# Six layer norms of a two-layer decoder step: mean and squares taken from shifted features while the last products run, in place of after them

## The chip, the cores and the metric

The kernel runs on one core of one Trainium2 chip. Its time is that of the whole program on the device, in microseconds. Three runs of the kernel before took 2835.37, 2836.15 and 2839.43 us; the median, 2836.15 us, is the time before. The profiled execution is a further one.

## What is computed

One inference step of a decoder with two layers, on 1024 prompt tokens and 32 sample tokens (8 sequences of 4), 1024 features wide:

```
layer 0: mixer = sparse attention (an indexer scores all keys, the 256 best are kept)
layer 1: mixer = gated causal convolution of width 3
each layer:
  y = layer_norm(ALPHA * y + mixer(y))
  a, g = split(y @ w_up);  h = silu(causal_conv3(a) + b) * g       # 2816 features
  y = layer_norm(ALPHA * y + h @ w_down)

layer_norm(x): mu = mean(x); var = mean((x - mu)**2)
               (x - mu) * rsqrt(var + 1e-5) * gain + bias
```

All of it is fp32. The change bears on the first three of the four layer norms; the last one (`last_norm`) is another function and stays.

## The kernel before, in words

**Precision.** Each large operand is split into two fp32r parts, `hi` (ScalarE, a rounding copy, L129) and `lo` (the rest, by a subtraction on VectorE or GpSimd, L130). A product is three passes: `wh·xh`, `wh·xl`, `wl·xh` (L732, L733, L735 in `product`, L724). Weights come by DMA into `raw` on SP's queue and are split right before use (`unit`, L714). Matmuls with `allones`, in the norms, are in full fp32.

**Layout.** Activations lie with features on the partitions: `r` is 128 x 8 blocks x tokens, so a layer norm sums over 8 blocks and over the 128 partitions. Tokens are in two groups: A, 512 prompt tokens, and B, the other 512 with the 32 sample tokens, 544 columns in two halves of 272.

**Order.** First come the projections and the indexer, then the attention of A. Then A goes through the attention's output projection (`out_proj`, L794), norm 0, the FFN of layer 0, norm 1, the conv mixer, norm 2, and the beginning of the FFN of layer 1. In that time the scores, the top-k and the attention of B are a background generator (L1284): `weave` (L79 to L85) issues pieces of it between A's products according to costs written by hand, and `drain` issues what is left. After the background, B runs its own `out_proj`, norm 0, FFN, norm 1, conv, norm 2 and FFN, and the rest of A's last FFN is cut into chunks (`CHUNKS`, L19; `N0, N1, N2 = 2, 3, 4`, L49) that are issued around B's norms as cover (`stage`, L1314; L1346 to L1360): features 0 to 7 before B starts, 8 to 11 around norm 0, 12 to 15 around norm 1, 16 to 21 around norm 2.

`pipeline` (L863) runs a chunk: the up products of its features (`up`), the first up of the next chunk, then the down products (`down`, L751): for each of the 8 output blocks `d` a product over the chunk's features, which VectorE adds into `r` (L773), or, in the first chunk, combines with the residual (L782, L813). The framework orders each engine's instructions ahead of time by a priority list; on the chip every engine runs its own in that order, and waits on semaphores.

**The norm** (`norm`, L974) is called after the last `down`:

1. GpSimd adds the blocks of `r` into `s` as they come (L982, L984; in B the last one on VectorE, L987). In A the last block goes into the matmul by itself.
2. PE sums over partitions with a matrix of ones (`sums`, L957, L962), ScalarE scales that to the mean (L990).
3. VectorE subtracts it from two blocks at a time (L994), ScalarE squares them (L996), GpSimd adds the two squares (L997); in B further adds bring all into one row (L1003).
4. PE turns the squares by matmuls with one column into a variance for each token, tokens on the partitions (L1013, L1017): a column for each 128 tokens and term, four terms in A, one in B. VectorE takes it out (L1023), GpSimd raises it to the power -1/2 (L968), VectorE does a Newton step (L969 to L971).
5. VectorE makes diagonal matrices of the result (L1028), PE spreads them over the partitions (L1033), ScalarE copies (L1035), VectorE multiplies (L1038), ScalarE applies gain and bias (L1041), and the new `xh`, `xl` are split off, the second and fourth `xl` on GpSimd.

While A's part runs, PSUM is tight (`single` is true): the products and the norm's sums take turns in two banks. Later there are three double banks for products and two others for the norm.

## Time and profile before

| what | value |
|---|---|
| runs of the kernel before, median | 2836.15 us |
| the profiled execution, time | 2832.02 us |
| its span, first to last instruction | 2830.2 us |
| mean granted TensorE clock over the span | 0.968 |
| instructions in it | 43977 |
| moved by DMA | 271.57 MB |

The profile is of one execution. Its span leaves out what lies before the first and after the last instruction, 1.8 us here, and the execution is 4.1 us faster than the median. PE is TensorE, DVE VectorE, ACT ScalarE, POOL GpSimd, SP the engine that issues most DMAs. An instruction is named by engine, line of the kernel and tiles, output first: `mm<-xhA,wh` is a product in group A. PE's busy time covers instructions that overlap; the granted clock is 1.00 at the upper level and 0.5 at the lower.

### The profile page before, as it was taken

How to read it: one execution, taken by the hardware profiler on the slowest of the kernel's cores; microseconds unless marked ns; L12 is line 12 of the kernel's file. 1: busy time of each engine (PE TensorE's matmuls, PEld its weight loads, DVE VectorE, ACT ScalarE, POOL GpSimd, SP SyncE). 2: the span in 40 equal slices, each digit the busy share in tenths (PEclk: the TensorE clock that was granted, in tenths of full speed). 3: DMA queues.
4: the chain of work that ended last, by engine and by line, in shares of the span. 5: the costliest groups of instructions: out<-in, count | busy, mean ns of one | idle time of the engine just before them, and what ended most of it. 6: DMA issues, size and time to landing. Idle time of an engine off the chain costs nothing.

```text
span 2830.2 us, 43977 instructions
## 1 busy us (share of the span) xinstructions
PE 2708.3 (96%) x16441; PEld 2422.8 (86%) x16441; DVE 1807.1 (64%) x3348; ACT 1329.6 (47%) x2305; POOL 702.1 (25%) x1040
## 2 busy tenths in 40 slices
PE   7999989899999989998999999999999998999997
PEld 7789977688777778886879899999989987999996
DVE  3466576998889855677754755445664566754446
ACT  3576774766886553356632533332332234432323
POOL 4455742111222353135201300000310031200001
PEclk8999999899999979999999999999999999999999
DMA  4245543133223323322244232323222322333332
GB/s 146 63 140 137 152 140 118 53 97 91 80 78 86 106 76 125 107 71 64 65 136 142 71 90 84 89 84 108 85 83 68 99 79 75 119 90 87 89 93 72
DMA packets 144021, 271.57 MB, mean 96 GB/s; under 512 B 27712, under 2 KB 74240, under 8 KB 143168
## 3 DMA queue, kind: packets, MB, share of 16 engines
q1 hardware_dynamic: 141120, 259.32, 31.0%
q0 software_dynamic: 2688, 9.44, 1.0%
q8 instruction: 130, 2.13, 0.3%
q14 instruction: 83, 0.68, 0.1%
HBM read 245.34 MB, written 23.36 MB: 95 GB/s over the span
## 4 chain that ended last, share of the span: by engine, by line
PE 77%; DVE 9%; ACT 5%; issue 4%; DMA 3%; POOL 2%; SPq 0%; ACTq 0%; DVEq 0%; POOLq 0%
PE mm L732 15%; PE mm L735 15%; PE mm L733 15%; PE m L735 6%; PE m L732 6%; PE m L733 6%; PE pv L587 2%; DVE wl L130 2%; PE tr L583 2%; PE pj L186 2%; PE pj L187 1%; PE pj L185 1%; PE ix L319 1%; ACT tkb L422 1%; PE ix L567 1%
## 5 line engine op out<-in xcount | busy, mean ns | idle before, releaser
L129 ACT ACTIVATE wh<-raw 128x1024 fp32r<-128x1024 f32 (+2 forms) x456 | 383.7, 842 | 806.0 <-PE mm L733 605.7
L130 DVE TENSOR_TENSOR wl<-raw,wh 128x1024 fp32r<-128x1024 f32 (+2 forms) x456 | 467.8, 1027 | 280.5 <-ACT wh L129 275.5
L732 PE MATMUL mm<-xhB,wh 128*128 128x272 f32 x1920 | 520.2, 290 | 6.2 <-ACT xhB L129 6.2
L733 PE MATMUL mm<-xlB,wh 128*128 128x272 f32 x1920 | 519.0, 288 | 2.5 <-DVE xlB L130 2.5
L735 PE MATMUL mm<-xhB,wl 128*128 128x272 f32 x1920 | 398.0, 289 | 0.0
L732 PEld LDWEIGHTS mm<-xhB,wh 128*128 128x128 f32 x1920 | 363.7, 190 | 7.3 <-ACT xhB L129 7.0
L733 PEld LDWEIGHTS mm<-xlB,wh 128*128 128x128 f32 x1920 | 362.7, 189 | 3.3 <-DVE xlB L130 3.0
L735 PEld LDWEIGHTS mm<-xhB,wl 128*128 128x128 f32 x1920 | 301.2, 189 | 0.0
L732 PE MATMUL m<-xhA,wh 128*128 128x512 f32 x736 | 294.0, 402 | 6.1 <-DVE h L857 2.4
L733 PE MATMUL m<-xlA,wh 128*128 128x512 f32 x736 | 293.6, 399 | 3.3 <-DVE xlA L130 3.0
L735 PE MATMUL m<-xhA,wl 128*128 128x512 f32 x736 | 293.7, 399 | 1.5 <-DVE wl L130 1.4
L732 PE MATMUL mm<-hh,wh 128*128 128x272 f32 (+1 forms) x928 | 269.6, 307 | 8.9 <-DVE r L773 8.0
L733 PE MATMUL mm<-hl,wh 128*128 128x272 f32 (+1 forms) x928 | 268.6, 305 | 0.0
L735 PE MATMUL mm<-hh,wl 128*128 128x272 f32 (+1 forms) x928 | 220.1, 306 | 2.2 <-DVE wl L130 2.2
L732 PEld LDWEIGHTS mm<-hh,wh 128*128 128x128 f32 x928 | 175.1, 189 | 16.7 <-DVE r L773 5.9
L733 PEld LDWEIGHTS mm<-hl,wh 128*128 128x128 f32 x928 | 175.4, 189 | 6.1
L834 POOL COPY ffn_outs<-ext 128x2 f32<-128x2 f32 x44 | 25.7, 584 | 601.0 <-ACT ext L903 600.9
L732 PEld LDWEIGHTS m<-xhA,wh 128*128 128x128 f32 x736 | 140.3, 192 | 36.7 <-DVE h L857 3.0
L733 PEld LDWEIGHTS m<-xlA,wh 128*128 128x128 f32 x736 | 140.2, 191 | 33.5 <-DVE xlA L130 4.2
L735 PEld LDWEIGHTS m<-xhA,wl 128*128 128x128 f32 x736 | 140.4, 191 | 31.4 <-DVE wl L130 2.5
L185 PE MATMUL pj<-W,X 128*128 128x368 f32 (+3 forms) x480 | 154.9, 325 | 12.1 <-ACT W L129 10.3
L773 DVE TENSOR_TENSOR r<-r,mm 128x544 f32<-128x544 f32 (+1 forms) x120 | 85.1, 710 | 121.9 <-PE mm L735 121.5
(369 smaller groups left out, 5960.9 us busy)
## 6 DMA issues: line engine op xcount, KB each, us to landing
raw<-w_up SPq DMA_DIRECT2D x176, 512.0 KB, 3.6
raw<-w_down SPq DMA_DIRECT2D x128, 256.0 KB, 2.6
raw<-w_ci SPq DMA_DIRECT2D x48, 512.0 KB, 3.6
X<-xp SPq DMA_DIRECT2D x24, 512.0 KB, 3.2
raw<-w_down SPq DMA_DIRECT2D x64, 192.0 KB, 2.4
qr<-dQ SPq DMA_DIRECT2D x64, 128.0 KB, 2.9
raw<-w_ao SPq DMA_DIRECT2D x16, 512.0 KB, 3.6
raw<-w_co SPq DMA_DIRECT2D x32, 256.0 KB, 2.7
```

The costliest lines, as they stand in the source:

```text
L129: nc.scalar.activation(hi, src, AF.Copy)
L130: (nc.gpsimd if pool else nc.vector).tensor_sub(lo, src, hi.bitcast(F32))
L185: nc.tensor.matmul(p, xh[:, k, :], hi, start=(k == 0), stop=False)
L186: nc.tensor.matmul(p, xh[:, k, :], lo, start=False, stop=False)
L187: nc.tensor.matmul(p, xl[:, k, :], hi, start=False, stop=(k == 7))
L319: nc.tensor.matmul(p, Q[:, h % 8, :], K[z][:, c:c + m], start=(z == 0), stop=(z == 1))
L583: nc.tensor.transpose(p[:, 128 * j:128 * j + 128], es[j][:, 128 * c:128 * c + 128], self.ident)
L587: nc.tensor.matmul(o, V[:, c], pp[:, z], start=(c == 0 and z == 0), stop=(c == i and z == 1))
L732: nc.tensor.matmul(o, wh[:, k, :], xh[:, c:c + m], start=(k == 0), stop=False)
L733: nc.tensor.matmul(o, wh[:, k, :], xl[:, c:c + m], start=False, stop=False)
L735: nc.tensor.matmul(o, wl[:, k, :], xh[:, c:c + m], start=False, stop=(k == n - 1))
L773: nc.vector.tensor_add(rv, rv, acc)
```

## The change

A class `Norm` takes the place of `norm`. `down` calls its `each` after every block `d` of the last chunk. Up to `d = 3` GpSimd sums the blocks 0 to 3; ScalarE rounds that sum to fp32r, and one pass of a matmul gives `c`, about the mean of those 512 features, the same value in all partitions. From `d = 4` on the blocks are shifted by `c` on VectorE: the finished ones two at a time, the unfinished ones before their last product is added. ScalarE squares shifted pairs into one tile `B`, GpSimd adds the squares into `acc` and the shifted blocks into `s1`. In `finish` the remaining mean `mb` comes from `s1` by an fp32 matmul, and the variance columns have twice as many PSUM columns: sums of `s1`, and squares from `acc`, `B[:, 0]` and `B[:, 1]`. The variance is mean square less squared mean. The four pairs then lose `mb`, and the rest of the norm is as before. In `out_proj` the residual is always added in the only chunk, so blocks from 5 on are shifted inside `base`.

Beside it: `out_proj` loads the attention output in four DMAs of two blocks into `r` itself, not in eight through the two-buffer tile `h`; the background generator is put on the list when the last query tile of A is done, and what was on the list before is finished ahead of A's last two key heads; A's last FFN is cut as `LAST`, seven chunks, six features of which come before B starts, 6 to 9 around norm 0, 10 to 15 (two chunks) around norm 1.

```diff
-N0, N1, N2 = 2, 3, 4
+
+LAST = ((0, 4), (4, 2), (6, 4), (10, 4), (14, 2), (16, 3), (19, 3))
+N0, N1, N2 = 2, 3, 5
...
+class Norm:
+    def __init__(self, net, g, m):
+        self.net, self.g, self.m = net, g, m
+        self.nc, self.n = net.nc, g.n
+    def row(self, dt=F32):
+        return self.net.wk.tile([128, 544], dt, name="nr", bufs=2)[:, :self.n]
+    def two(self):
+        return self.net.wk.tile([128, 2, 544], F32, name="n", bufs=self.net.nn)[:, :, :self.n]
+    def bc(self, x):
+        return x[:, None, :].to_broadcast([128, 2, self.n])
+    def each(self, d, r, fresh):
+        nc, n = self.nc, self.n
+        one = lambda d: r[:, d, :n]
+        pair = lambda d: r[:, d:d + 2, :n]
+        shift = lambda x: nc.vector.tensor_sub(x, x, self.bc(self.c) if len(x.shape) == 3 else self.c)
+        if d == 1:
+            self.A = self.two()
+            self.acc, self.s1 = self.A[:, 0], self.A[:, 1]
+            self.s = self.acc
+            nc.gpsimd.tensor_add(self.s, one(0), one(1))
+        elif d == 2:
+            nc.gpsimd.tensor_add(self.s, self.s, one(2))
+        elif d == 3:
+            self.sr = self.row(F32R)
+            nc.gpsimd.tensor_add(self.s, self.s, one(3))
+            nc.scalar.activation(self.sr, self.s, AF.Copy)
+        elif d == 4:
+            self.c = self.row()
+            for p, cols in self.net.sums(self.g, [self.sr], self.net.allonesr):
+                nc.scalar.activation(self.c[:, cols], p, AF.Copy, scale=1.0 / 512.0)
+            shift(pair(0))
+            shift(one(4) if fresh else pair(4))
+            nc.vector.scalar_tensor_tensor(self.s1, self.c, -4.0, self.s, op0=OP.mult, op1=OP.add)
+            self.B = self.two()
+            nc.scalar.activation(self.B, pair(0), AF.Square)
+            nc.gpsimd.tensor_add(self.acc, self.B[:, 0], self.B[:, 1])
+        elif d == 5:
+            if not fresh:
+                shift(pair(6))
+            for e in (4, 5):
+                nc.gpsimd.tensor_add(self.s1, self.s1, one(e))
+            self.squares(pair(4))
+            shift(pair(2))
+        elif d == 6:
+            nc.gpsimd.tensor_add(self.s1, self.s1, one(6))
+            self.squares(pair(2))
+        elif d == 7:
+            nc.vector.tensor_add(self.s1, self.s1, one(7))
+            nc.scalar.activation(self.B, pair(6), AF.Square)
+    def squares(self, x):
+        self.nc.scalar.activation(self.B, x, AF.Square)
+        for z in range(2):
+            self.nc.gpsimd.tensor_add(self.acc, self.acc, self.B[:, z])
+    def finish(self, r):
+        nc, net, g, n, m = self.nc, self.net, self.g, self.n, self.m
+        pair = lambda d: r[:, d:d + 2, :n]
+        mb = self.row()
+        for p, cols in net.sums(g, [self.s1], net.allones):
+            nc.scalar.activation(mb[:, cols], p, AF.Copy, scale=1.0 / 1024.0)
+        tiles = [(i, c, min(128, n - c)) for i, c in enumerate(range(0, n, 128))]
+        nt = len(tiles)
+        var = net.bank()
+        nc.tensor.matmul(var[:, :2 * nt], net.allones, net.zeros[:, :2 * nt], start=True, stop=False)
+        terms = [(self.s1, nt), (self.acc, 0), (self.B[:, 0], 0), (self.B[:, 1], 0)]
+        for i, (x, o) in enumerate(terms):
+            for t, c, k in tiles[::-1]:
+                nc.tensor.matmul(var[:k, o + t:o + t + 1], x[:, c:c + k], net.allones[:, 0:1], start=False,
+                                 stop=(i == 3 and t == 0))
+        sm = net.wk.tile([128, 4, 6], F32, name="mv", bufs=2)[:, :, :nt]
+        if g.b:
+            nc.gpsimd.memset(sm, 1.0)
+        for rows, c in ((128, slice(0, 4)), (32, slice(4, 5)))[:1 + g.b]:
+            v, mean, q = sm[:rows, 0, c], sm[:rows, 3, c], sm[:rows, 2, c]
+            nc.vector.tensor_scalar(mean, var[:rows, nt:2 * nt][:, c], 1.0 / 1024.0, None, op0=OP.mult)
+            nc.vector.scalar_tensor_tensor(q, mean, -1.0, mean, op0=OP.mult, op1=OP.mult)
+            nc.vector.scalar_tensor_tensor(v, var[:rows, c], 1.0 / 1024.0, q, op0=OP.mult, op1=OP.add)
+            nc.vector.tensor_scalar(v, v, EPS, None, op0=OP.add)
+        y = net.rsqrt(sm[:, 0], sm[:, 1], sm[:, 2])
+        yb = diag = self.row()
+        for t, c, k in tiles:
+            nc.vector.tensor_scalar(diag[:k, c:c + k], net.ident[:k, :k], y[:k, t:t + 1], None, op0=OP.mult)
+        for d in range(0, 8, 2):
+            nc.vector.tensor_sub(pair(d), pair(d), self.bc(mb))
+        for c0 in range(0, n, 512):
+            p = net.bank()
+            for t, c, k in tiles:
+                if c0 <= c < c0 + 512:
+                    nc.tensor.matmul(p[:, c - c0:c - c0 + k], net.allones[:k], diag[:k, c:c + k], start=True, stop=True)
+            m_ = min(512, n - c0)
+            nc.scalar.activation(yb[:, c0:c0 + m_], p[:, :m_], AF.Copy)
+        xh, xl = net.new_x(g)
+        for d in range(0, 8, 2):
+            nc.vector.tensor_mul(pair(d), pair(d), self.bc(yb))
+            t = self.two()
+            for z in range(2):
+                nc.scalar.activation(t[:, z], r[:, d + z, :n], AF.Identity, scale=net.ln[:, m, d + z, 0:1],
+                                     bias=net.ln[:, m, d + z, 1:2])
+            net.split(xh[:, d:d + 2, :], xl[:, d:d + 2, :], t, pool=d % 4 == 2)
...
-    def down(self, g, r, hh, hl, n, src, base, apart=False):
+    def down(self, g, r, hh, hl, n, src, base, apart=False, norm=None):
...
                 base(d, rv, acc)
+            if norm:
+                norm.each(d, r, base is not None)
...
-    def out_proj(self, g):
+    def out_proj(self, g, norm):
         nc, a = self.nc, self.a
         hh, hl = self.new_x(g)
-        for d in range(8):
-            raw = self.wk.tile([128, 560], F32, name="h", bufs=2)[:, :g.n]
-            nc.sync.dma_start(raw, self.do[g.name][:, d, :])
-            self.split(hh[:, d, :], hl[:, d, :], raw)
         r = self.new_r()
+        for d in range(0, 8, 2):
+            raw = r[:, d:d + 2, :g.n]
+            nc.sync.dma_start(raw, self.do[g.name][:, d:d + 2, :])
+            self.split(hh[:, d:d + 2, :], hl[:, d:d + 2, :], raw)
 
         def base(d, rv, acc):
             xr = self.wk.tile([128, 560], F32, name="cv", bufs=2)
@@ -810,12 +928,17 @@
             else:
                 nc.sync.dma_start(xr[:, :512].rearrange("p (t c) -> p t c", t=4),
                                   a["xp"][0:4, :, d, :].rearrange("t p c -> p t c"))
-            nc.vector.scalar_tensor_tensor(rv, g.view(xr[:, :g.n]), ALPHA, acc, op0=OP.mult, op1=OP.add)
+            if d < 5:
+                nc.vector.scalar_tensor_tensor(rv, g.view(xr[:, :g.n]), ALPHA, acc, op0=OP.mult, op1=OP.add)
+            else:
+                nc.vector.scalar_tensor_tensor(rv, g.view(xr[:, :g.n]), ALPHA, g.view(norm.c), op0=OP.mult,
+                                               op1=OP.subtract)
+                nc.vector.tensor_add(rv, rv, acc)
...
-    def sums(self, g, terms):
+    def sums(self, g, terms, ones):
...
-                self.nc.tensor.matmul(p, self.allones, t[:, s], start=(i == 0), stop=(i == len(terms) - 1))
+                self.nc.tensor.matmul(p, ones, t[:, s], start=(i == 0), stop=(i == len(terms) - 1))
...
-        self.allones = pc.tile([128, 128], F32, name="allones")
-        nc.vector.memset(self.allones, 1.0)
-        self.zeros = pc.tile([128, 8], F32, name="zeros")
+        self.allonesr = pc.tile([128, 128], F32R, name="allones")
+        self.allones = self.allonesr.bitcast(F32)
+        nc.vector.tensor_scalar(self.allonesr, self.ident, 0.0, 1.0, op0=OP.mult, op1=OP.add)
+        self.zeros = pc.tile([128, 10], F32, name="zeros")
...
+            self.bg.append(background())
...
             self.weave(cost)
+        self.finish(1)
         for cost in together((self.attend(GA, T1, range(4), (2, 3)), A1), (second(), A2)):
             self.weave(cost)
-        self.drain()
-        self.bg = [background()]
         close("p1")
...
-        r = self.result(self.out_proj(GA))
-        self.norm(GA, r, 0)
+        norm = Norm(self, GA, 0)
+        norm.finish(self.result(self.out_proj(GA, norm)))
         self.fill(F0)
...
-        r = self.result(self.ffn(GA, 0))
-        self.norm(GA, r, 1)
-        r = self.result(self.conv(GA))
-        self.norm(GA, r, 2)
+        norm = Norm(self, GA, 1)
+        norm.finish(self.result(self.ffn(GA, 0, norm=norm)))
+        norm = Norm(self, GA, 2)
+        norm.finish(self.result(self.conv(GA, norm)))
         self.fill(F0)
 
-        G = self.ffn(GA, 1, CHUNKS[:N0])
+        G = self.ffn(GA, 1, LAST[:N0])
...
-        G = stage("oB", self.out_proj(GB), G, rA.append)
+        norms = [Norm(self, GB, m) for m in range(3)]
+        G = stage("oB", self.out_proj(GB, norms[0]), G, rA.append)
         r = self.result(G)
-        G = self.ffn(GA, 1, CHUNKS[N0:N1], rA[0])
+        G = self.ffn(GA, 1, LAST[N0:N1], rA[0])
         self.until(G, "begun")
-        self.norm(GB, r, 0)
+        norms[0].finish(r)
         self.until(G, "tail")
         new_r("b")
-        G = stage("fB0", self.ffn(GB, 0), G, lambda r: None)
-        F = self.ffn(GA, 1, CHUNKS[N1:N2], rA[0])
-        G = stage("fA1b", F, G, lambda r: self.norm(GB, r, 1))
-        G = stage("cB", self.conv(GB), G, lambda r: None)
-        F = self.ffn(GA, 1, CHUNKS[N2:], rA[0])
-        G = stage("fA1c", F, G, lambda r: self.norm(GB, r, 2))
+        G = stage("fB0", self.ffn(GB, 0, norm=norms[1]), G, lambda r: None)
+        F = self.ffn(GA, 1, LAST[N1:N2], rA[0])
+        G = stage("fA1b", F, G, norms[1].finish)
+        G = stage("cB", self.conv(GB, norms[2]), G, lambda r: None)
+        F = self.ffn(GA, 1, LAST[N2:], rA[0])
+        G = stage("fA1c", F, G, norms[2].finish)
```

## Rows read from the trace of the kernel before

**Rows 1.** The page, first part: an engine's busy time, its share of the span, its instructions.
```profile
PE 2708.3 (96%) x16441; PEld 2422.8 (86%) x16441; DVE 1807.1 (64%) x3348; ACT 1329.6 (47%) x2305; POOL 702.1 (25%) x1040
```
**Rows 2.** Busy time by stretches: the stretch in us from the start of the span, its length, then the busy time (and number of instructions) of PE, PEld, DVE, ACT and POOL, the granted share of the TensorE clock, the DMA share, and GB/s. Two stretches for each norm, in order A0, A1, A2, B0, B1, B2: from the last `r` to line 1023, and from there until products run densely.
```profile
474.30:494.20 19.90, 16.21 (x71) 13.32 (x69) 17.52 (x14) 11.14 (x22) 8.15 (x4) 0.77 0.18 57
494.20:531.50 37.30, 26.97 (x90) 19.40 (x88) 33.54 (x63) 28.70 (x52) 7.95 (x11) 0.71 0.06 21
990.30:1018.60 28.30, 23.34 (x104) 19.75 (x103) 14.00 (x18) 13.49 (x17) 15.96 (x24) 0.62 0.25 75
1018.60:1045.50 26.90, 23.62 (x103) 17.91 (x102) 15.25 (x28) 14.06 (x22) 19.66 (x26) 0.77 0.25 79
1283.50:1307.60 24.10, 17.62 (x89) 13.92 (x87) 18.44 (x34) 12.73 (x18) 10.62 (x8) 0.86 0.23 62
1307.60:1345.50 37.90, 31.03 (x145) 22.80 (x143) 28.70 (x64) 28.41 (x45) 21.43 (x15) 0.95 0.13 39
1547.70:1582.30 34.60, 34.60 (x158) 28.25 (x157) 24.51 (x23) 13.65 (x19) 12.71 (x10) 1.00 0.29 82
1582.30:1608.00 25.70, 23.23 (x130) 20.45 (x129) 21.81 (x30) 16.69 (x23) 10.25 (x10) 0.93 0.12 34
2030.30:2057.00 26.70, 26.70 (x123) 21.84 (x123) 21.61 (x21) 11.51 (x15) 13.79 (x10) 1.00 0.34 101
2057.00:2085.00 28.00, 21.83 (x118) 19.45 (x118) 20.58 (x27) 15.74 (x21) 8.17 (x8) 0.82 0.10 28
2302.50:2329.30 26.80, 26.80 (x123) 21.85 (x122) 21.59 (x20) 10.91 (x15) 13.27 (x9) 1.00 0.22 66
2329.30:2364.00 34.70, 26.78 (x111) 20.93 (x110) 26.50 (x39) 18.74 (x28) 9.52 (x6) 0.95 0.23 69
```
**Rows 3.** The chain of waits, for PE: what waited for what, us in total, times, the longest in us.
```profile
PE mm L732 <- DVE r L773: 8.0, 3, 3.0
PE m L1017 <- POOL n L997: 6.9, 5, 4.9
PE mm L732 <- ACT xhB L129: 6.2, 2, 5.4
```
**Rows 4.** The norm's instructions by line: how many, the shortest, median and longest duration in ns, the first and last start in us, the shapes; in the last row the number, busy us and the mean in ns.
```profile
L984 POOL TENSOR_TENSOR nr<-nr,r x30: 1252/1587/2447, 443.2 to 2299.6; 128x512 f32<-128x512 f32 x15, 128x544 f32<-128x544 f32 x15
L990 ACT ACTIVATE nr<-m x3: 597/602/604, 477.5 to 1289.9; 128x512 f32<-128x512 f32 x3
L994 DVE TENSOR_TENSOR r<-r,nr x24: 1217/1284/2452, 478.2 to 2313.0; 128x1024 f32<-128x1024 f32 x12, 128x1088 f32<-128x1088 f32 x12
L996 ACT ACTIVATE n<-r x24: 1041/1078/1120, 479.5 to 2320.0; 128x1024 f32<-128x1024 f32 x12, 128x1088 f32<-128x1088 f32 x12
L997 POOL TENSOR_TENSOR n<-n x24: 1266/1848/2412, 480.6 to 2322.1; 128x512 f32<-128x512 f32 x12, 128x544 f32<-128x544 f32 x12
L1023 DVE TENSOR_SCALAR mv<-m 128x4 f32<-128x4 f32 x3 | 0.5, 153 | 0.0
```
**Rows 5.** The instructions that write `r` in the last products ahead of A0, A1, A2 (its last six), B1 and B2, in the columns of rows 4; and the weight splits of units of three features, all of them, with busy us, mean ns and idle time before.
```profile
L813 DVE SCALAR_TENSOR_TENSOR r<-cv,m x8: 680/688/691, 434.3 to 473.6; 128x512 f32<-128x512 f32 x8
L773 DVE TENSOR_TENSOR r<-r,m x8: 667/675/687, 966.8 to 989.6; 128x512 f32<-128x512 f32 x8
L773 DVE TENSOR_TENSOR r<-r,m x6: 675/682/689, 1263.3 to 1282.8; 128x512 f32<-128x512 f32 x6
L773 DVE TENSOR_TENSOR r<-r,mm x8: 706/722/722, 2013.8 to 2029.6; 128x544 f32<-128x544 f32 x8
L773 DVE TENSOR_TENSOR r<-r,mm x8: 709/722/722, 2280.7 to 2301.7; 128x544 f32<-128x544 f32 x8
L130 DVE TENSOR_TENSOR wl<-raw,wh 128x384 fp32r<-128x384 f32 x56 | 41.3, 737 | 19.1 <-ACT wh L129 19.1
```
**Rows 6.** PE in order of time: start in us, length in us, line, operation, shapes, number merged into the row, and the idle time before it where there was any; the last row in the columns of rows 4.
```profile
473.39 1.02 PE L962 MATMUL m<-nr,allones 128*128 128x512 f32 x2
...
2055.23 1.21 PE L1017 MATMUL tr<-allones,nr 128*32 128x1 f32 x10
2056.30 0.47 PE L735 MATMUL mm<-xhA,wl 128*128 128x512 f32 x1
2056.61 0.39 PE L732 MATMUL mm<-xhA,wh 128*128 128x512 f32 x1
2056.84 0.40 PE L733 MATMUL mm<-xlA,wh 128*128 128x512 f32 x1
...
2071.93 0.82 PE L732 MATMUL mm<-xhB,wh 128*128 128x272 f32 x2 [5.37 <-ACT xhB L129]
L962 PEld LDWEIGHTS tr<-nr,allones x12: 187/188/193, 1557.5 to 2308.3; 128*128 128x128 f32 x12
```
**Rows 7.** The loads of the attention output (L799): who waited for them, us, times.
```profile
  ACT xhB L129: 9.9, 4
  ACT xhA L129: 8.3, 4
```
**Rows 8.** First, in the columns of rows 4, the background's last kind of product (`pv`); then, in the columns of rows 2, the stretch from there to the end of A's last up product, and the one between the norms B1 and B2.
```profile
L587 PE MATMUL pv<-pp,V x288: 387/394/803, 262.8 to 1432.7; 128*128 128x512 f32 x144
1433.00:1471.50 38.50, 38.31 (x169) 31.29 (x167) 22.22 (x31) 13.33 (x19) 1.89 (x6) 1.00 0.47 157
2080.00:2320.00 240.00, 240.00 (x1731) 230.44 (x1730) 123.31 (x178) 61.11 (x79) 33.59 (x43) 1.00 0.30 89
```

More of the change, by code (lines that the diff above doesn't have):

```diff
@@ L817, in out_proj @@
         yield from self.down(g, r, [hh[:, k, :] for k in range(8)], [hl[:, k, :] for k in range(8)], 8,
-                             lambda d: a["w_ao"][d], base)
+                             lambda d: a["w_ao"][d], base, norm=norm)
         return r
@@ L885, in pipeline, with ffn @@
         return r
-    def ffn(self, g, l, chunks=CHUNKS, r=None, apart=False):
+    def ffn(self, g, l, chunks=CHUNKS, r=None, apart=False, norm=None):
         nc, a = self.nc, self.a
@@ L915, in down, with conv @@
             return self.down(g, r, [h[0] for h in H], [h[1] for h in H], nf,
-                             lambda d: a["w_down"][l, d, :, f0:f0 + nf, :], base, apart and f0 + nf == NFF)
+                             lambda d: a["w_down"][l, d, :, f0:f0 + nf, :], base, apart and f0 + nf == NFF,
+                             norm if f0 + nf == NFF else None)
         return self.pipeline(g, up, chunks, down, get_r, base, 10.3)
-    def conv(self, g):
+    def conv(self, g, norm):
         nc, a = self.nc, self.a
@@ L949, in down @@
         def down(r, H, f0, nf, base):
-            return self.down(g, r, [h[0] for h in H], [h[1] for h in H], nf, lambda d: a["w_co"][d, :, f0:f0 + nf, :], base)
+            return self.down(g, r, [h[0] for h in H], [h[1] for h in H], nf, lambda d: a["w_co"][d, :, f0:f0 + nf, :], base,
+                             norm=norm if f0 == 4 else None)
         return self.pipeline(g, up, ((0, 4), (4, 4)), down, self.new_r, self.residual(g), 15.5)
```

66 lines of the change are left out of this document (removed).

## The prediction

> **What bounds the kernel now.** I read the page's busy shares first [rows 1]: TensorE is busy 2708.3 of 2830.2 us, so there is something to win only where it stands or its granted clock is low. The table by stretches [rows 2] shows where: around the six layer norms. Call them A0, A1, A2 (group A, after the attention projection, the first FFN and the conv) and B0, B1, B2. Each is cut in two at the instruction that takes the variance out of PSUM (L1023): the front half runs from the last `r` to there, the back half from there until products run densely again. A stretch loses TensorE's idle time plus the time at the lower of its two clock levels (1.2 instead of 2.4 GHz; one minus the granted share, times the length; an upper estimate, since idle time at the low clock counts twice). The three A fronts lose 3.7 + 5.0 + 6.5 us idle and 4.6 + 10.8 + 3.4 us by the clock: 33.8 us in 72.3, or 0.47 per us. The A backs lose 39.4 us in 102.1. The B fronts lose nothing, because products of A cover them; the B backs lose 4.3, 11.2 and 9.6 us. The chain of waits for PE [rows 3] names the causes: the variance matmuls wait for GpSimd's sums of squares (6.9 us), the next product for the normed features (6.2 us), and A's last products for `r` (8.0 us). Outside the norms PE runs near its pitch, so the total is PE's work plus what it loses at such places.
>
> **The change, part by part.**
>
> *The front half.* Today the order after the last `r` is: finish the sum, matmul, mean, four subtractions (1.28 us), four squares (1.08 us), GpSimd adds (median 1.85 us), then the variance [rows 4]. The change does three of the four squares and most sums while products run, on features shifted by a mean of the first four blocks. After the last `r` there remain one VectorE add (0.72 us), one square, the fp32 sum matmul, and the variance columns. What is late next is GpSimd. From the fourth `r` on the chain is an add 1.59, rounding 0.6, matmul 0.23, copy 0.6, shift 1.28, square 1.08 [rows 4]: 5.4 us; then eight adds in a row on GpSimd at 1.85 = 14.8 us (10.1 at the shortest, 19.3 at the longest add of the row), then the last square 1.1: 21.3 us (16.6 to 25.8). Against it stand four products. Their pitch is 5.6 us in A0, 3.3 in A1, 3.9 in A2, 2.3 in B1, 3.0 in B2 [rows 5], so GpSimd trails the last `r` by 0, 8.3, 5.7, 12.3 and 9.3 us. Five variance columns cost PE 1.07 us [rows 6], so four 0.86; the last two terms add 1.7 to 2.1 us, and three more small VectorE operations at 0.15 each 0.5. Where GpSimd doesn't trail, the path is 0.7 + 0.9 + four terms of 0.9 to 1.1 + 0.5, some 6.5 us. New fronts: A0 6.5, A1 10.9, A2 8.3, against 19.9, 28.3 and 24.1: 46.6 us shorter. At 0.47 per us that is **-21.9 us**. Bounds: -17.7 with all adds at their longest; -8 if the background work alone sets the pace (rival 1).
>
> What the row shows of GpSimd beside VectorE: the same subtraction takes 1.22 us at its shortest and 2.45 at its longest, the same add 1.27 and 2.41 [rows 4], so each grows by about the other's length. The Trainium skill, SBUF — State Buffer, section Who interferes with whom, says that a VectorE operation with two SBUF inputs and a GpSimd one that reads SBUF exclude each other for a whole instruction; the trace agrees (2.45 against 1.22). It speaks against this change, which puts GpSimd's adds beside shifts and weight splits: by it the adds go nearer 2.41, and the sum would be 2816 instead of 2811.
>
> *The back half* keeps its steps (power, diagonal, broadcast, multiply, affine, split). Four subtractions of the exact remaining mean are added (4 x 1.28 = 5.1 us per norm). They need only the sum matmul, so they fit beside the variance columns, the power and the diagonal; I cost them at nothing. Without that cover they are on the path: 5.1 us a norm, in A at about 0.4 lost per us, some 6 us in all.
>
> *Group B.* The A chunks are recut: 8 features before B instead of 8 become 6, the stage that covers B1 gets 6 in two chunks instead of 4. An up projection is 48 matmuls of 0.23 us = 11 us [rows 6]. In B1 the first product came at 2071.9, 41 us after the last `r`, and 5.4 us after A's products ran out; two more ups and a down chunk add some 44 us of cover and the path is 11 us shorter, so of 11.2 us lost 2 stay: **-9**. In B2 the cover is the same, but the path is 14 us shorter, so that the multiplies and splits fall beside up products rather than beside downs that wait for `r` (part of the 8.0 us in [rows 3]): half of 9.6, **-5** (0 to -8). B0: **-2.5** of 4.3.
>
> *More work for PE.* B's variance has 20 columns instead of 5: 15 x 0.214 = 3.2 us a norm, plus two rounded half sums at about half of 0.23. In A one fp32 sum (two passes, 1.02 us in the row, 0.87 without the end that the next matmul overlaps) becomes a rounded one at 0.23. 3 x 3.46 - 3 x 0.64 = **+8.5**. In B this is paid in full, since PE has work there.
>
> *Late products.* In the last four products VectorE gets four shifts (1.28 to 2.45), one combination (some 0.7, like an `r` add) and its `r` adds and weight splits (0.72 and 0.74 each) [rows 4, 5]: 11.8 to 16.4 us, against 9.0 in B1 and 12 in B2. Behind the shifts on VectorE stand the `r` adds, and PE waits for those. B1 +3 (0 to 7.4), B2 +0.5 (0 to 4.4), A +1.5 where the mean's sum takes one of two PSUM banks: **+5** (0 to 13).
>
> *Edits with one answer.* The attention output is loaded in four DMAs straight into `r` instead of eight through two buffers, which made ScalarE wait 8.3 and 9.9 us [rows 7]. SP carries four transfers fewer per group; each is twice as large and stands before the first weights. The first product waits for weights as well: 0 (-3 to +3). Three more VectorE operations in the projection, and eight more `r` adds and smaller weight splits from the seventh chunk, lie where VectorE is half idle (123 of 240 us) [rows 8]; uncovered, about 8 us of VectorE. The background is begun a few steps earlier; its work was already hoisted there, so 0. It ended at about 1433 us, with 38.5 us of dense A products behind it [rows 8]; 33 us of these move, so the step into B keeps some 27 us of cover: 0 (-2 to +4).
>
> Sum: -21.9 - 9 - 5 - 2.5 + 8.5 + 5 = **-24.9 us**. The profiled execution took 2832.0 us, 4.1 below the median of the runs; 2807 by it, **2811** by the median.
>
> **The rivals.**
>
> 1. *The background sets the pace.* In the A0 and A2 fronts VectorE is busy 17.5 of 19.9 and 18.4 of 24.1 us [rows 2], mostly with background; a shorter norm only moves that work. Against: in A1 VectorE is busy only 14.0 of 28.3. Then the A gain is -8, the sum -11: 2825. Chance 0.18.
> 2. *PE stands at the variance matmuls* (the slower one). PE works in order. If GpSimd's adds go at 2.41, the last square is 4.5 us later than reckoned; ScalarE, in order too, holds weight splits behind the squares that wait. PE stood there already in A (5 waits, 6.9 us). From 4.1 us a norm the gain is gone; at 6 us in all six it is 36 us, sum +11: 2847. For it: eight adds now follow one another. Against: B's fronts show no such wait today. Chance 0.11.
> 3. *The A backs shorten too*, if the background stands elsewhere and more of it is ready: a third of 39.4 us, 13 more: 2798. Chance 0.15.
> 4. *The sums don't start earlier*: in B0 the first sum matmul came some 10 us after the last `r`, behind an up product in PE's order (1557.5 against 1547.7 in [rows 2, 6]). If the same holds back the new matmuls, B gains nothing: -21.9 + 8.5 + 5 = -8.4: 2828. Chance 0.06.
>
> **How the numbers follow.** The forecast, 2800 to 2824, has 0.50. Range 2790 to 2837: it takes in rivals 1 and 4 and the nearer half of 3, and leaves out rival 2 and the far part of 3. A measurement can tell about 0.2%, 5.7 us, from no change. Faster by more: the forecast (less a tail of 0.05), rival 3 and most of 1 and 4, 0.78. Within it: that tail and the ends of rivals 1, 2 and 4, 0.11. Slower: 0.11.
>
> **What would show it.** Fronts of about 7, 11 and 8 us in A, 15 and 12 in B1 and B2; PE busy through B1; 40 variance matmuls a norm in B at the old pitch; GpSimd without a gap from the fifth product to the last square. Long PE waits at the variance matmuls, `r` adds late in B1, or A stretches as long as before would make it wrong.

## The result, and the profile after

The changed kernel took **2861.95 us** (four runs, 2861.62 to 2862.38); the kernel before took 2835.76 beside it. The ratio is 1.0101 with a 95% interval of 1.0083 to 1.0119: **slower by 1%**, where 2811 was forecast. The kernel before differs between chips (2831.6 to 2835.8), so below each kernel is compared by its ratio to the runs of before on its own chip, with the 95% interval in brackets; 0.1% is 2.8 us. Places inside a kernel are read from its one profiled execution.

The page of the changed kernel [against rows 1]: PE is busy 12.3 us longer in a span that is 30.2 us longer.

```profile
PE 2720.6 (95%) x16534; PEld 2437.3 (85%) x16534; DVE 1840.0 (64%) x3417; ACT 1336.0 (47%) x2318; POOL 702.0 (25%) x1040
```

The fronts of the norms, from the last `r` to the instruction that takes the variance out (L164 now), in the order A0, A1, A2, B0, B1, B2 and the columns of [rows 2]:

```profile
476.90:487.30 10.40, 9.03 (x45) 7.96 (x46) 10.22 (x10) 3.67 (x8) 1.27 (x1) 0.74 0.29 93
986.10:1000.80 14.70, 9.86 (x39) 8.71 (x40) 11.85 (x12) 5.55 (x8) 6.42 (x6) 0.53 0.40 138
1270.60:1286.90 16.30, 13.26 (x49) 10.70 (x50) 14.53 (x32) 6.58 (x11) 9.72 (x8) 0.60 0.26 81
1527.10:1549.30 22.20, 22.20 (x115) 19.09 (x115) 12.19 (x13) 6.21 (x9) 2.86 (x4) 0.95 0.25 72
2020.50:2039.90 19.40, 19.40 (x96) 16.92 (x95) 11.91 (x15) 6.02 (x8) 7.76 (x7) 0.85 0.24 81
2333.60:2353.60 20.00, 20.00 (x97) 17.33 (x96) 12.65 (x13) 5.51 (x8) 9.74 (x7) 0.84 0.24 75
```

Every front is shorter: those of A by 9.5, 13.6 and 7.8 us, 30.9 of the 46.6 that were forecast. The norm did get shorter where I looked, and the kernel slower. The chain of waits, for PE [against rows 3], shows what came in its place (left out between them are the indexer's row, 15.2 us around A0 against 10.9 before, and a row of the first projections):

```profile
PE mm L848 <- ACT wh L245: 17.9, 3, 15.5
...
PE mm L848 <- DVE r L889: 12.8, 3, 7.2
...
PE m L1087 <- DVE n L134: 7.9, 3, 6.3
```

The last row is A's, 6.3 us of it in A1: the sum matmul waits there for the last add into `s1`. Before, the variance matmuls waited, 6.9 us [rows 3].

**Ahead of the front.** The `r` row is for the most part the last products of B1 (7.18 us) and B2 (4.06). These are VectorE's instructions in order of time in B1 (start, length, line, operation, idle time before), then some of PE, GpSimd and ScalarE in the same stretch:

```profile
2004.10 0.72 DVE L889 TENSOR_TENSOR r<-r,mm 128x544 f32<-128x544 f32 x1 [0.81 <-PE mm L851]
2004.73 0.55 DVE L246 TENSOR_TENSOR wl<-raw,wh 128x384 fp32r<-128x384 f32 x1
2007.20 1.23 DVE L246 TENSOR_TENSOR wl<-raw,wh 128x1024 fp32r<-128x1024 f32 x1 [1.91 <-ACT wh L245]
2008.50 2.49 DVE L101 TENSOR_TENSOR r<-r,nr 128x1088 f32<-128x1088 f32 x2
2010.91 0.72 DVE L119 SCALAR_TENSOR_TENSOR n<-nr,n 128x544 f32<-128x544 f32 x1
2011.55 3.62 DVE L101 TENSOR_TENSOR r<-r,nr 128x1088 f32<-128x1088 f32 x2
2015.09 2.35 DVE L246 TENSOR_TENSOR wl<-raw,wh 128x1024 fp32r<-128x1024 f32 x1
2017.36 0.71 DVE L889 TENSOR_TENSOR r<-r,mm 128x544 f32<-128x544 f32 x1
...
2007.39 0.41 PE L1087 MATMUL tr<-nr,allones 128*128 128x272 f32 x2
...
2018.21 0.77 PE L848 MATMUL mm<-xhA,wh 128*128 128x512 f32 x1 [7.18 <-DVE r L889]
...
2002.94 1.56 POOL L111 TENSOR_TENSOR n<-n,r 128x544 f32<-128x544 f32 x1
2011.78 2.25 POOL L122 TENSOR_TENSOR n<-n 128x544 f32<-128x544 f32 x1 [7.27 <-DVE n L119]
...
2004.54 0.66 ACT L112 ACTIVATE nr<-n 128x544 fp32r<-128x544 f32 x1 [0.17 <-POOL n L111]
2007.71 0.69 ACT L116 ACTIVATE nr<-tr 128x272 f32<-128x272 f32 x2 [0.55 <-PE tr L1087]
```

The fifth `r` add (2004.10) and the sixth (2017.36) stand 13.3 us apart, at a product's pitch of 2.3 [rows 5]. The early mean is there only at 2008.40, at the end of its copy. Then VectorE does four shifts and the combination (6.7 us, 2008.50 to 2015.17) and a weight split (2.35 us) before it comes to that add. The finished products wait in PSUM for the `r` adds; PE, with no free buffer for the next one, stands for 7.18 us. GpSimd, which was to be busy without a gap, waits 7.27 us too. In all six norms the `r` adds have a hole of 9 to 13 us at this place, where the pitch is about 6 us in A0 and B0 and 2 to 4 us in the others. So the last `r`, from which the front is measured, comes later, and part of what the front gained is lost ahead of it. The instructions that raise the variance to the power -1/2 ("power instructions" below) of A0 and A2 stand 804.4 us apart (488.1 to 1292.5), against 813.5 before: 9 us, though the fronts of A1 and A2 are 21 us shorter.

**Where B starts.** The first row of the waits is for the most part one gap of 15.5 us. SP's queue, ScalarE and PE there:

```profile
1448.28 0.38 SPq L711 DMA_DIRECT2D doB<-ou  x1
1450.69 2.03 SPq L918 DMA_DIRECT2D r<-doB  x4
1452.77 0.49 SPq L836 DMA_DIRECT2D raw<-w_down  x1
...
1456.89 2.27 ACT L245 ACTIVATE xhB<-r 128x1088 fp32r<-128x1088 f32 x2 [9.51 <-DMA r<-doB]
1459.42 1.11 ACT L245 ACTIVATE xhB<-r 128x1088 fp32r<-128x1088 f32 x1 [0.25 <-DMA r<-doB]
1460.80 1.11 ACT L245 ACTIVATE xhB<-r 128x1088 fp32r<-128x1088 f32 x1 [0.27 <-DMA r<-doB]
1461.81 0.40 ACT L245 ACTIVATE wh<-raw 128x256 fp32r<-128x256 f32 x1
...
1462.27 0.80 PE L848 MATMUL mm<-hh,wh 128*128 128x512 f32 x1 [15.52 <-ACT wh L245]
```

The product that PE waits for, `mm<-hh,wh`, is A's own and needs nothing of B. But its weights are loaded and split behind the four loads of the attention output and the four splits of `xhB`, in both queues, and these wait for the background's last store (`doB<-ou`, 1448.28). Before, A's dense products lay there [rows 8]; now A's last up product ends at 1440.2, 6.5 us ahead of the background's last product (1446.7), and the same 38.5 us hold 22.27 us of PE:

```profile
1433.00:1471.50 38.50, 22.27 (x92) 16.98 (x91) 17.42 (x27) 13.97 (x22) 0.28 (x2) 0.73 0.36 124
```

**The variance columns.** A column is two matmul instructions. The 40 of B1 take 6.36 us, against 1.21 for the 10 of before [rows 6]. The stretches before, during and behind them, all with PE busy throughout; the clock is the third number from the end:

```profile
2032.85 6.36 PE L157 MATMUL tr<-allones,n 128*32 128x1 f32 x40
...
2025.00:2032.80 7.80, 7.80 (x37) 6.41 (x35) 3.34 (x3) 4.25 (x7) 3.58 (x2) 1.00 0.18 67
2032.85:2039.00 6.15, 6.15 (x41) 6.04 (x40) 6.08 (x7) 0.39 (x1) 0.23 (x1) 0.67 0.15 33
2039.20:2045.00 5.80, 5.80 (x15) 4.54 (x15) 3.75 (x18) 1.19 (x2) 1.19 (x2) 0.50 0.11 44
```

### The profile page after: what moved, and what is told of

It is laid out like the page before. It is cut to its first block, busy times and chain, and to the rows that moved or that the text cites. A ratio compares the mean times of both kernels' runs of the same rounds, so it can differ in the third digit from the quotient of the medians.

```text
span 2860.4 us, 44247 instructions
## 1 busy us (share of the span) xinstructions
PE 2720.6 (95%) x16534; PEld 2437.3 (85%) x16534; DVE 1840.0 (64%) x3417; ACT 1336.0 (47%) x2318; POOL 702.0 (25%) x1040
## 3 DMA queue, kind: packets, MB, share of 16 engines
q1 hardware_dynamic: 141120, 259.32, 30.9%
## 4 chain that ended last, share of the span: by engine, by line
PE 76%; DVE 9%; ACT 5%; DMA 4%; issue 4%; POOL 1%; SPq 0%; ACTq 0%; DVEq 0%; POOLq 0%
PE mm L848 15%; PE mm L849 15%; PE mm L851 15%; PE m L848 5%; PE m L849 5%; PE m L851 5%; PE pj L301 2%; PE pj L302 2%; PE pj L303 2%; PE pv L703 2%; DVE wl L246 1%; PE tr L699 1%; PE ix L435 1%; ACT tkb L538 1%; PE ix L683 1%
## 5 line engine op out<-in xcount | busy, mean ns | idle before, releaser
L245 ACT ACTIVATE wh<-raw 128x1024 fp32r<-128x1024 f32 (+3 forms) x464 | 385.2, 831 | 777.7 <-PE mm L849 592.9
L246 DVE TENSOR_TENSOR wl<-raw,wh 128x1024 fp32r<-128x1024 f32 (+3 forms) x464 | 466.0, 1004 | 287.4 <-ACT wh L245 283.5
L848 PE MATMUL m<-xhA,wh 128*128 128x512 f32 x704 | 281.3, 401 | 7.3 <-ACT xhA L245 5.8
L848 PE MATMUL mm<-hh,wh 128*128 128x272 f32 (+1 forms) x928 | 269.2, 306 | 17.1 <-ACT wh L245 15.5
L851 PE MATMUL m<-xhA,wl 128*128 128x512 f32 x704 | 279.3, 397 | 2.2 <-DVE wl L246 2.0
L849 PE MATMUL m<-xlA,wh 128*128 128x512 f32 x704 | 280.0, 398 | 0.0
L301 PE MATMUL pj<-W,X 128*128 128x368 f32 (+3 forms) x480 | 153.9, 323 | 13.2 <-ACT W L245 11.7
L848 PEld LDWEIGHTS m<-xhA,wh 128*128 128x128 f32 x704 | 134.3, 191 | 35.1 <-ACT xhA L245 6.3
L851 PEld LDWEIGHTS m<-xhA,wl 128*128 128x128 f32 x704 | 133.7, 190 | 31.1 <-DVE wl L246 4.7
L303 PE MATMUL pj<-W,X 128*128 128x368 f32 (+3 forms) x480 | 154.6, 323 | 4.2 <-DVE X L246 4.2
```

Of the source, the lines that this page charges most:

```text
L245: nc.scalar.activation(hi, src, AF.Copy)
L246: (nc.gpsimd if pool else nc.vector).tensor_sub(lo, src, hi.bitcast(F32))
L301: nc.tensor.matmul(p, xh[:, k, :], hi, start=(k == 0), stop=False)
L303: nc.tensor.matmul(p, xl[:, k, :], hi, start=False, stop=(k == 7))
L848: nc.tensor.matmul(o, wh[:, k, :], xh[:, c:c + m], start=(k == 0), stop=False)
L849: nc.tensor.matmul(o, wh[:, k, :], xl[:, c:c + m], start=False, stop=False)
```

## The experiments

My theory after the result was that three things cost, each in its own place: the early mean with its shifts (S), B's start (by its loads, L, or by too little cover, C), and the columns (P). The rival was that the recut, the loads and the background spoil a norm that is good in itself. Twelve kernels were run.

**Undoing one part.** e1 sets `LAST = CHUNKS`, `N0, N1, N2 = 2, 3, 4`. e2 brings the old loads back, e4 the old `norm`, e5 the old place of the background:

```
 e2 out_proj:
+        for d in range(8):
+            raw = self.wk.tile([128, 560], F32, name="h", bufs=2)[:, :g.n]
...
-        for d in range(0, 8, 2):
-            raw = r[:, d:d + 2, :g.n]
...
 e5:
-            self.bg.append(background())
...
-        self.finish(1)
...
+        self.drain()
+        self.bg = [background()]
```

> The change with the old cut of A's last FFN (features 0 to 7 before B, then 4, 4, 6). Theory C (cover): in the changed kernel PE stands 15.5 us at the step into B because only two features of A's products are left to run while the attention output is written, loaded and split; with four features and two more ups behind the background that gap falls to about 2 us, B1 loses two ups of cover and stands some 3 us more: 2850 us (2845 to 2856). Theory L (loads): the four loads in a row and their four splits ahead of the weight splits on ScalarE make the gap, whatever the cover: 2862, gap 12 us or more.

e1 took 2848.5 us, ratio 1.0051 (1.0033 to 1.0069): 14 us came back, as theory C had it. The gap at B's start is gone (no wait over 1.1 us is left there); those of 7.15 us in B1 and 4.04 in B2 stay.

> The change with the old eight loads of the attention output through the two-buffer tile. Theory C: the gap at the step into B stays within 3 us of 15.5, time 2862 (2858 to 2866). Theory L: the weight split comes ahead of the later splits on ScalarE and the gap falls to 5 us or less: 2851.

e2 took 2844.5 us, ratio 1.0043 (1.0026 to 1.0059): 16 us came back, and the gap falls to 1.4 us, while the chunks are the new ones. With eight loads through a two-buffer tile, SP takes A's weights in between, and so does ScalarE with their splits:

```profile
1444.98 0.44 SPq L917 DMA_DIRECT2D h<-doB  x1
...
1445.99 0.41 SPq L836 DMA_DIRECT2D raw<-w_down  x1
```

So in the changed kernel either undoing removes the gap. But e2 has more cover as well: its background ends earlier (last product at 1433.0), and A's up products run on to 1443.9. Where the cover is used up in both, the old loads leave a gap of 9.9 us and the new ones 16.2 (e6 and e3, below). By that the order in the queues is worth some 6 us, and the rest of what e2 closes is cover; why the background ends earlier in e2 isn't shown.

> The change with the old norm, so that the chunks, the loads and the early background are left of it. Theory: the new norm costs (PE's added work about 15 us, late blocks) and the rest costs too (the step into B about 15 us, less some 8 us for B1's cover): 2843 us (2838 to 2850). Rival N: the norm is the whole cost, the rest gains: 2828 to 2836. Rival R: the rest is the whole cost and the norm gains about what it costs: 2858 or more.

e4 took 2835.4 us, ratio 1.0011 (1.0000 to 1.0021), less than my theory and within the time of rival N, though the rest gains nothing either. With the old norm the other edits together are worth about nothing: a gap of 5.1 us stands at B's start, and B1's gap of 5.4 us is gone. Their price comes with the new norm.

> The changed kernel (2862) with the background queued and drained as before. Theory that the background's earlier start costs or gives nothing by itself: 2858 to 2866, and the 15.5 us gap of PE at the step into B stays. Theory that the earlier place of the background is what makes the step into B bare (its end moves against the A products): the gap shrinks below 8 us and the time is 2850 to 2856. Theory that the earlier start does help A's stages: slower, 2868 or more.

e5 took 2854.6 us, ratio 1.0074 (1.0059 to 1.0088). The gap at B's start stays (15.3 us), so neither theory's picture holds, but 0.27% came back. The interval still touches that of the changed kernel; e10 and e11 below test it again.

**The shift.** e3 leaves out the early mean and the shifts: `s1` sums the raw blocks, and the squares are of raw features. Without the shift the variance is the difference of two larger numbers; what that costs in accuracy is outside these runs, which are about time.

```
-            self.s = self.acc
-            nc.gpsimd.tensor_add(self.s, one(0), one(1))
...
-            self.c = self.row()
-            for p, cols in self.net.sums(self.g, [self.sr], self.net.allonesr):
-                nc.scalar.activation(self.c[:, cols], p, AF.Copy, scale=1.0 / 512.0)
-            shift(pair(0))
-            shift(one(4) if fresh else pair(4))
-            nc.vector.scalar_tensor_tensor(self.s1, self.c, -4.0, self.s, op0=OP.mult, op1=OP.add)
...
-            if not fresh:
-                shift(pair(6))
...
-            shift(pair(2))
```

> The change without the shift: the early mean of four blocks and the subtractions of it are left out, sums and squares are taken of the features as they are (the variance is still mean square less squared mean). Theory S: in the changed kernel the fifth block's add into r comes 9 to 13 us after the fourth's in all six norms, since on VectorE it stands behind the wait for the early mean and the shifts of four pairs, and PE then waits for accumulators (7.2 us before B1, 4.1 before B2); without the shift these two waits go, the blocks come at their pitch, and the path of each norm is 5 to 9 us shorter: 2842 us (2836 to 2850). Rival: what costs is PE's added work and the step into B alone; then the path is shorter but nothing waits for it: 2858 or more.

e3 took 2830.7 us, ratio 0.9992 (0.9982 to 1.0003): **31 us came back**, more than the 20 that theory S had. The gaps in B1 and B2 are gone; the one at B's start stays, 16.2 us:

```profile
PE mm L834 <- ACT wh L231: 18.4, 3, 16.2
```

In the profiled executions 12.5 of the 31 us are there by B0's power instruction, and 25 come between those of B0 and B2; 6.5 are lost again behind them. The stretch from B0 to B2 in the changed kernel, the part of it right behind the 7.18 us wait, and the stretch from B0 to B2 in e3:

```profile
1552.50:2356.20 803.70, 790.58 (x5573) 755.40 (x5573) 438.59 (x634) 253.39 (x382) 100.95 (x171) 0.98 0.29 85
2018.20:2024.00 5.80, 5.79 (x19) 4.66 (x20) 3.18 (x4) 1.07 (x1) 5.79 (x4) 0.73 0.60 184
...
1540.00:2318.40 778.40, 776.86 (x5555) 744.09 (x5555) 423.47 (x618) 248.38 (x373) 98.63 (x169) 1.00 0.30 88
```

PE stands 13.1 us in the first and 1.5 in the last, and it is busy 13.7 us longer with nearly the same matmuls, at a granted clock of 0.98 against 1.00. So the waits are about half of what the shift costs in B; the other half is matmuls at the lower clock, behind the waits (0.73 above) and at the variance columns.

e8 keeps the shifts and shifts by zeros, so that nothing waits for a mean:

```
+            self.c = self.row()
+            nc.gpsimd.memset(self.c, 0.0)
...
-            self.c = self.row()
-            for p, cols in self.net.sums(self.g, [self.sr], self.net.allonesr):
-                nc.scalar.activation(self.c[:, cols], p, AF.Copy, scale=1.0 / 512.0)
```

> The changed kernel with the shift by a row of zeros in place of the early mean: the shifts on VectorE stay, all of them, but nothing waits for a rounded sum, its matmul and the copy (the result is the same in exact arithmetic). The run without any shift gave 31 us back. Theory W, the wait for the early mean ahead of the shifts is what makes the fifth r add late: 2835 to 2842, PE's gap in B1 under 2 us. Theory D, the shifts' own time on VectorE ahead of that add is the cost: the gap in B1 only falls from 7.2 to about 3.5 us (the 3.7 us between the fourth r add and the first shift go, the 8.9 us of shifts stay), and the time is 2848 to 2856. Neither: 2858 or more.

e8 took 2835.8 us, ratio 1.0013 (1.0004 to 1.0023): 25 of the 31 us came back, as theory W had it, and no gap over 2.4 us is left in B1 and B2. The wait for the mean, with what follows from it, costs most; the shifts' own time some 6 us. VectorE around the same adds in B1, the fourth `r` add at 1991.11, the fifth at 1992.21 and the sixth at 1996.89:

```profile
1988.27 1.28 DVE L101 TENSOR_TENSOR r<-r,nr 128x1088 f32<-128x1088 f32 x1
...
1991.11 0.71 DVE L886 TENSOR_TENSOR r<-r,mm 128x544 f32<-128x544 f32 x1
...
1992.21 0.71 DVE L886 TENSOR_TENSOR r<-r,mm 128x544 f32<-128x544 f32 x1
...
1993.85 1.28 DVE L101 TENSOR_TENSOR r<-r,nr 128x1088 f32<-128x1088 f32 x1
...
1995.69 1.28 DVE L101 TENSOR_TENSOR r<-r,nr 128x1088 f32<-128x1088 f32 x1
1996.89 0.71 DVE L886 TENSOR_TENSOR r<-r,mm 128x544 f32<-128x544 f32 x1
```

The first shift now lies ahead of the fourth add, two others between the fifth and the sixth. The wait and the bunching are one effect here: because the mean comes late, four shifts come at once. How much of the 25 us is waiting and how much is order, this run doesn't tell.

**Putting parts together.** e6 is e3 with e2's loads; e7 adds, in B alone, two VectorE adds that bring the last squares into `acc`, so that 10 columns do instead of 20:

```
+        if g.b:
+            for z in range(2):
+                nc.vector.tensor_add(self.acc, self.acc, self.B[:, z])
+            terms = terms[:2]
...
```

> The changed kernel without the early mean and the shifts (sums and squares of the raw features) and with the old eight loads. Theory that the two costs add (shifts 31 us by the run without them, loads 15 to 17 us by the run with the old loads, in different places): about 2815, the gap of PE at the step into B under 3 us, faster than the kernel before by 0.6 to 0.8%. Theory that the two overlap, because the step into B is limited by the background's end whichever way the loads go: 2826 to 2832, no faster than without the shifts alone.

e6 took 2820.5 us, ratio 0.9958 (0.9945 to 0.9972), 0.34% or 10 us below e3 and between the two theories. A gap of 9.9 us at B's start remains: the parts add, but not in full. With the faster A its up products end at 1434.4, ahead of the background's last product (1437.6), where in e2 they ended 11 us behind it.

> As the run without shifts and with the old loads, and in group B VectorE adds the last two rows of squares into the sum of squares, so that 10 variance columns are made instead of 20. The 40 matmuls of a B norm took 6.3 us of PE, so half are 3.1 us. Theory that PE pays for every column in B, since products stand ready: 3 x 3.1 = 9 us faster than that run. Theory that the two adds (0.7 to 1.3 us each) lengthen the path by as much where cover is thin, or that PE has slack there: within 3 us of it. If the adds delay the normed features in B0 and B2: up to 5 us slower.

e7 took 2811.8 us, ratio 0.9931 (0.9919 to 0.9944): 7.6 us below e6, of the 9 that were expected. PE pays for the columns in B.

> The version without shifts, with the old eight loads and the merged squares (2811.8, 0.9931 of the kernel before) and with the old chunks, so that two more features of A run before B starts and two fewer around B1. That version still has a gap of PE of 9.9 us where B starts. Theory that B's start waits for the end of the background and A's products are the cover: the two features (33 us of products) fill the gap, 8 to 10 us are saved there; what B1 loses without them is at most the 5.4 us that the kernel before lost there, less because its norm is shorter: 2803 to 2808. Theory that the cover is worth as much in B1: 2809 to 2815.

e9 took 2803.3 us, ratio 0.9895 (0.9878 to 0.9911): 10 us for closing the last gap, and B1 lost nothing by its smaller cover (no wait over 1.2 us there). For what is left with the old loads, the theory of too little cover (C) holds.

> The version without shifts, with the old eight loads and the merged squares, and with the background queued and drained as before. The changed kernel with the old background was 0.27% (7.6 us) nearer to the kernel before than the changed kernel is, with intervals that just overlap. Theory that the earlier queueing costs by itself: 2803 to 2807 on a chip where the kernel before takes 2831.6, and the gap at B's start is below 7 us. Theory that the difference was between executions: 2809 to 2815, the gap stays near 9.9 us.

e10 took 2807.6 us, ratio 0.9908 (0.9892 to 0.9924), 0.23% below e7 with the gap unchanged (10.1 us). So the old place of the background is faster again, beside another norm, but not at B's start.

> The kernel before with the new norm alone, without early mean and shifts and with the squares merged in group B: old loads, old chunks, old background. The version with the new background took 2803.3 (0.9895). The old background was worth 0.27% and 0.23% in the two pairs. Theory that this adds: 2796 to 2799, about 0.987. Theory that it was bound to the gap at B's start, which the old chunks have closed: 2801 to 2806, 0.989 to 0.990.

e11 took **2799.2 us, ratio 0.9875** (0.9859 to 0.9892): 35 us faster than the kernel before, the fastest of all, and as the theory had it that the background's old place adds. Against e9 that place is worth 0.20%, after 0.27% and 0.23%: in each pair the intervals touch, but all three pairs point the same way, by 6 to 8 us. The mean granted clock is higher with it each time (0.964 to 0.967, 0.971 to 0.975, 0.974 to 0.975); where that comes from is open. The one-column matmuls of B1 (half of its 20) and B2, and the longest wait for an `r` add in e11:

```profile
2022.35 1.21 PE L147 MATMUL tr<-allones,n 128*32 128x1 f32 x10
2281.09 2.34 PE L147 MATMUL tr<-allones,n 128*32 128x1 f32 x20
...
PE mm L838 <- DVE r L879: 4.5, 2, 2.7
```

> The kernel before with the new norm alone as the change has it, with early mean and shifts and 20 variance columns in B: old loads, old chunks, old background. Theory of a wait for the early mean, which stays: the gap before the fifth r add's product stays (about 7 us in B1, 4 in B2), the gap at B's start is under 3 us, and the changed kernel's 2862 falls by 15 (B's start) and 6 (background) to 2838 to 2844, no faster than the kernel before. Theory that the other edits were what spoiled a good norm (the prediction's sum without them): 2815 to 2825.

e12 took 2840.0 us, ratio 1.0019 (1.0003 to 1.0034). The shifted norm alone, with everything else as before, gains nothing, as the first theory had it; its chain of waits begins with

```profile
PE mm L848 <- DVE r L889: 14.5, 4, 7.2
```

So the rival is wrong in that the norm was good in itself. It is right in that the other edits cost, and only beside the new norm: 0.82% from e12 to the changed kernel, against 0.11% beside the old one (e4). From e11 to e12 there are 41 us, and the shift and ten columns in B are all that differs. The power instructions of A0 and A2 stand 812.6 us apart in e12 and 780.1 in e11, 813.5 before.

## Why the prediction was wrong

- **The step that failed first is "Late products", +5 (0 to 13).** It measured 31 us (e3), outside both bounds: 25 between B0 and B2, where I had put 3.5 for B1 and B2. I added up VectorE's work over four products (11.8 to 16.4 us against 9 to 12) and charged the excess. The sum was fair, the order was not looked at: the shifts can't begin until the mean is there, they come together, and the next `r` add stands behind them on VectorE. Of the wait that the change adds, for `c`, I never asked what is queued behind it, nor what PE's waits do to its clock. My text had named `r` adds late in B1 as a sign of error; that is what came.
- **The mean's chain** was put at 3.0 us from the fourth `r` to the shift (add, rounding, matmul, copy). It took 5.6 us in B1, from GpSimd's add at 2002.94 to the shift at 2008.50. Every link was about as priced but the matmul: its input is ready at 2005.20, and it starts at 2007.39, behind a product in PE's order. That is rival 4's mechanism, at another instruction.
- **"Some 27 us of cover stays" where B starts has a wrong sign in it.** 38.5 us less the 33 that move leaves 5.5, and a faster A brings the end of A's products nearer to the background's end; I added the 22 us instead of taking them off. What came is no cover at all: A's up products end 6.5 us ahead of the background. The background's last product ended between 1430 and 1447 us in every kernel with six A features before B, whichever norm A had (1437 with the old one). The price was some 15 us (e1, e2) instead of 0 (-2 to +4). "Loads: 0" holds only while A's products lie behind; without them the order of the loads is worth some 6 us (e3 against e6).
- **A's fronts, -21.9**: they took 10.4, 14.7 and 16.3 us, where 6.5, 10.9 and 8.3 were forecast. The mechanism was right and shows without the shift: the stretch from A0 to A2 is 33 us shorter in e11. With the shift it is 9 us shorter in the changed kernel and 1 in e12, because what the front gained was lost ahead of the last `r`; why the other edits make it 8 us shorter beside this norm isn't shown (beside the old one it is longer, 826.1 us in e4). I measured a front that starts at the last `r`, and the change moves the last `r`.
- **B1 -9, B2 -5**: B1's 5.4 us gap of before is gone in all kernels with the new norm, also with the old cover (e1, e9, e11, e12). The recut closes it too, with the old norm (e4). Either would have done, so beside the new norm the recut bought nothing there.
- **More work for PE, +8.5**: a term mis-sized by the clock. At the upper level the 40 matmuls take 4.61 us (e6), 3.4 more than 10, about as reckoned (3.2). But the granted clock falls during or behind them, which the sum didn't have: 1.6 us behind e6's, and in the changed kernel's B1 2.0 during and 2.9 behind. Halving them in three norms gave 7.6 us (e7), 6.8 of it by their length at the upper level, for 10 of the 15 added columns.
- **Contention** was weighed at 5 us. The shifts took 1.285 us in the median and 2.454 at the longest, GpSimd's adds beside them 2.25 (L122, above):

```profile
L101 DVE TENSOR_TENSOR r<-r,nr x22: 689/1285/2454, 458.8 to 2325.9; 128x1024 f32<-128x1024 f32 x10, 128x1088 f32<-128x1088 f32 x10, 128x512 f32<-128x512 f32 x1, 128x544 f32<-128x544 f32 x1
```

  By that the trace still agrees with the rule of the Trainium skill (SBUF — State Buffer, Who interferes with whom). But e8 has the same shifts and adds, with shifts of up to 3.408 us (median 1.278), and is 25 us faster, so contention isn't what made the kernel slow.
- **Background, 0**: 0.27%, 0.23% and 0.20% dearer in three pairs. Not explained.
- Rival 2, the slower one, had the right sign and a wrong place: PE stood not at the variance matmuls but earlier, at products that waited for `r` adds (and, in A1, at the sum matmul). Rival 1 was half right: the background's end does set the pace, but where B starts.

The balance in ratios to before: the norm without shift and with merged squares -1.25% (e11); the shift with the columns +1.44% (e12 against e11); chunks, loads and background +0.82% (after against e12). They add up to +1.01% because each is a step from one kernel to the next; in another order the parts would be other ones, as e4 shows.

## What to carry to other kernels

Work moved in among running products must be placed in the order of its engine: ask when its inputs come, and which instruction that frees a product's buffer stands behind it; a sum of busy times says nothing of that. Measure the path from a point that the change can't move, here the first `r` rather than the last. And an edit that costs nothing by itself (loads, a recut) may do so only because something slow covers it; when another part of the change takes that away, price them together.

## What the runs showed of the hardware

TensorE's granted clock fell at long rows of one-column fp32 matmuls though PE didn't idle. The stretch of e6's 40 and the one behind it, then the 20 and the 10 in e11 with the stretches behind them (the clock is the third number from the end; the upper level, 2.4 GHz, is 1.00, the lower, 1.2 GHz, 0.50):

```profile
2008.85:2013.40 4.55, 4.55 (x42) 4.45 (x41) 4.55 (x4) 1.07 (x2) 1.23 (x1) 0.99 0.00 0
2013.50:2018.00 4.50, 4.50 (x14) 3.60 (x15) 3.79 (x14) 1.35 (x2) 0.84 (x2) 0.64 0.40 117
...
2281.09:2283.40 2.31, 2.31 (x22) 2.26 (x22) 2.31 (x2) 0.00 (x0) 0.00 (x0) 0.99 0.00 0
2283.40:2288.00 4.60, 4.60 (x15) 3.65 (x15) 3.94 (x15) 1.54 (x2) 1.70 (x2) 0.63 0.11 27
...
2022.35:2023.60 1.25, 1.25 (x12) 1.24 (x12) 0.77 (x2) 0.41 (x1) 0.10 (x1) 1.00 0.59 203
2023.60:2028.00 4.40, 4.40 (x20) 3.64 (x20) 3.28 (x11) 1.78 (x3) 0.44 (x1) 1.00 0.32 86
```

Behind 40 and behind 20 the products run at a granted 0.63 to 0.64 for some 4.5 us, 1.6 to 1.7 us lost each time; behind 10 the clock stays at 1.00. In the changed kernel it fell already during the 40 (0.67) and stood at 0.50 behind them.
